# Two float32 products of an attention layer written as three split products each

## The chip, the cores and the metric

The kernel runs on one core of one Trainium2 chip. A time is the device time of one execution in microseconds, and what counts is the median of several runs. The profile is one execution of the same program, recorded by the hardware profiler; TensorE does the matrix products, VectorE, ScalarE and GpSimd the elementwise work, and SyncE issues most of the DMAs.

## The reference, cut to what matters

A sequence of 512 tokens with 16 learned meta tokens ahead of it (528 rows, width 2048) goes through two layers. Layer A is a gated linear recurrence. Layer B is forgetting attention with 16 heads of 128; its keys and values come from one projection of layer A's output. The change touches the part of layer B that follows:

```python
def fox_mix(h, g_norm, w_in, g_q, w_out, k, v, F, valid):
    u = rms_norm(h, g_norm) @ w_in
    q = rms_norm(u[..., :D_MODEL].reshape(bsz, L, FOX_HEADS, FOX_HDIM), g_q)
    z = u[..., D_MODEL:]
    ...
    for blk in range(Lp // Q_BLOCK):            # Q_BLOCK = 128
        s0 = blk * Q_BLOCK
        s1 = s0 + Q_BLOCK
        logits = jnp.einsum('bqhd,bkhd->bhqk', q[:, s0:s1], k[:, :s1]) * scale
        logits = logits + F[:, :, s0:s1, None] - F[:, :, None, :s1]
        logits = jnp.where(mask, logits, MASK_VALUE)
        p = jax.nn.softmax(logits, axis=-1)
        outs.append(jnp.einsum('bhqk,bkhd->bqhd', p, v[:, :s1]))
    ...
    return (o * jax.nn.silu(z)) @ w_out
```

All of it is float32.

## The kernel before

The kernel works with transposed activations: features on the 128 partitions, tokens along the free dimension. Its weights stream from HBM through `w_raw`, ScalarE rounds each piece to `w_hi` and VectorE subtracts to get `w_lo`, both in the type float32r, which is read as four bytes and takes one instruction for a product. A product in full accuracy is made of **three split products** that add up in PSUM: high x high, high x low, low x high. The activations have such a pair too (`sh`, `sl`). Everything large in the kernel is done so, in pieces of 256 to 512 moving columns. A product whose operands are plain float32 is recorded as two instructions.

Stages in time: layer A with its output projection, keys and values for layer B (to about 1405 us), the attention stage (to about 1826 us), and layer B's output projection. In the attention stage the projections for q and the gate z of head after head run through `run_ntiles`: for each of 32 slots 16 x 3 products of 512 columns (`pj`). Between them, in small pieces, stands the attention of an earlier head:

- `att_load` (L1672) loads kT (16+512 key columns) and the bias row Fb and, once the outputs of head h-2 are done, vtk and vc, which hold the values.
- `att_prep` (L1698) makes kh (ScalarE) and kl (GpSimd) of kT, the four masked bias tiles D (ScalarE, then GpSimd), the pair vh, vl of the values' first three blocks, and `v3`, a float32 copy of the fourth.
- `att_q` (L1723) scales the queries: the pair qh, ql for the query blocks 1 to 3, and `qg`, a float32 tile, for block 0; then the norms (`qy`).
- `att_blk` (L1765) does one query block i against its first 16 + 128(i+1) keys: scores into PSUM (`s`), bias (`lg`), softmax (`sm`, ScalarE's exponential), the transpose through DRAM (`py`, `pd`), and the parts PTh, PTl of the transposed weights. Block 0 has 144 columns, one float32 product of `qg` and kT. The blocks 1 to 3 have three split products for each piece of 272, 400, 272 and 256 columns.
- `att_o` (L1833) sums the outputs in PSUM (`o`): for each of three groups (vh x PTh, vl x PTh, vh x PTl) key blocks 0 to 2 against the query blocks that see them (512, 384 and 256 columns). The last key block meets only the last query block (128 columns): one float32 product of `v3` and `PT3`. A product with `vc` and Z adds the last 16 keys.

The order is written by a planner. All engines run what is issued to them in the written order. `do` writes an instruction only when a clock in the program, which adds up a price for each instruction, says that its operands are there; after each piece of a projection `tick` gives every waiting step a turn. In this clock a product of n columns costs TensorE 0.447 n + 3 ns in float32r and 1.9 n + 130 ns in float32, and from it comes where a step lands among the projections. When a slot begins that is two after a head's q slot, `att_o` of that head is put first in the list of steps.

All recorded instructions carry the line of a helper (L196), so rows are told apart by their tiles.

Of the kernel before, what the change touches and what calls it, by code (L numbers as in the profile page):

```python
# [14 lines left out]
P = 128  # L15
D = 2048
# [473 lines left out]
def trunk(  # L490
# [1207 lines left out]
    def att_prep(h):  # L1698
# [16 lines left out]
        while "vt" not in a:  # L1715
            yield
        a["v"] = yield from parts(a["vt"].rearrange("p (g b f) -> p g b f", g=4, f=32)[:, :, :3], "v", 384, ge, 2)
        v3 = tb.tile([P, P], F32, name="v3", tag="v3", bufs=2)
        yield from do(act, v3.rearrange("p (g f) -> p g f", f=32),
                      a["vt"].rearrange("p (g b f) -> p g b f", g=4, f=32)[:, :, 3], AF.Copy)  # L1720
        a["v3"] = v3

    def att_q(h, uq):  # L1723
# [7 lines left out]
        qh = tb.tile([P, 3 * P], F32R, name="qh", tag="qh")  # L1731
        ql = tb.tile([P, 3 * P], F32R, name="ql", tag="ql")
        yield from do(act, qh, uq[:, P:], AF.Identity, scale=g)
        yield from do(ve.scalar_tensor_tensor, ql, uq[:, P:], g, qh.bitcast(F32), ALU.mult, ALU.subtract)
        qg = tb.tile([P, P], F32, name="qg", tag="qg")
        yield from do(ge.tensor_scalar, qg, uq[:, :P], g, None, ALU.mult)
        free_u("buq")
        a.update(qg=qg, q=(qh, ql))
# [26 lines left out]
    def att_blk(h, i):  # L1765
        a = A[h]
        last = A.get(h - 1, {})
        kT, d = a["kT"], a["D"][i]
# [9 lines left out]
        for c0, c1 in cuts:  # L1778
            psS = ps.tile([P, 512], F32, name="s", tag="s", bufs=3)
            pss_.append(psS)  # L1780
            if i == 0:
                yield from do(te.matmul, psS[:, :n], lhsT=a["qg"], rhs=kT[:, :n], start=True, stop=True)
            else:
                qh, ql = (t[:, (i - 1) * P:i * P] for t in a["q"])
                kh, kl = (t[:, c0:c1] for t in a["k"])
                for j, (qq, kk) in enumerate(((qh, kh), (qh, kl), (ql, kh))):
                    yield from do(te.matmul, psS[:, :c1 - c0], lhsT=qq, rhs=kk, start=j == 0, stop=j == 2)
# [31 lines left out]
        if "PTh" not in a:  # L1819
            a["PTh"] = tb.tile([P, 4, 384], F32R, name="PTh", tag="PTh", bufs=1)  # L1820
            a["PTl"] = tb.tile([P, 4, 384], F32R, name="PTl", tag="PTl", bufs=1)
            a["PT3"] = tb.tile([P, P], F32, name="PT3", tag="PT3", bufs=1)
# [6 lines left out]
        if i == 3:  # L1829
            yield from do(act, a["PT3"].rearrange("p (g f) -> p g f", f=32), src[:, :, 3], AF.Copy)  # L1830
        a["fin"].add(i)

    def att_o(h):  # L1833
        a = A[h]
        while "v3" not in a or len(a["fin"]) < 4:
            yield
        PTh, PTl, PT3 = a["PTh"], a["PTl"], a["PT3"]
        while not all(te.matmul.fits((), {"lhsT": v, "rhs": w}) for v, w in (
                (a["v"][0], PTh), (a["v"][1], PTl), (a["v3"], PT3), (a["vc"], Z[h % 2]))):
# [270 lines left out]
```

## Time and profile before

| | us |
|---|---|
| median of 3 runs | 2013.81 |
| lowest, highest | 2009.59, 2014.51 |
| the profiled execution's own time | 2009.89 |
| its span, first to last instruction | 2008.2 |
| TensorE busy | 1980.4 |
| VectorE, ScalarE, GpSimd busy | 1573.1, 1000.5, 319.6 |
| granted TensorE clock, mean | 0.997 of 2.4 GHz |

The recorded duration of a product runs from its start to the end of its way through the array, and the next product starts long before that end. What a product costs is therefore read from start to start. Rows named PEld are loads of the stationary operand; one stands before each product.

### The profile page before, as it was taken

What the parts mean: (1) busy time and instruction counts of PE and PEld (TensorE: products, weight loads), DVE (VectorE), ACT (ScalarE), POOL (GpSimd) and SP (SyncE); (2) the same over time, 40 slices, a digit from 0 to 9 for tenths busy, and PEclk for the clock granted to TensorE, in tenths of its full rate; (3) what the DMA queues carried; (4) which work ended last, traced back from release to release, by engine and by line L of the source; (5) the groups of instructions that cost most, each with busy time, mean ns of one, the idle gap of its engine ahead of it and who ended that gap; (6) DMA issues with size and microseconds to landing.
All of it is one profiled execution on the core that took longest, in us unless ns stands there. A gap on an engine that the chain in (4) does not pass through costs nothing.

```text
span 2008.2 us, 39614 instructions
## 1 busy us (share of the span) xinstructions
PE 1980.4 (99%) x14604; PEld 1851.0 (92%) x14604; DVE 1573.1 (78%) x3153; ACT 1000.5 (50%) x1869; POOL 319.6 (16%) x429
## 2 busy tenths in 40 slices
PE   8999999999999999999999999999999999999999
PEld 7999999999999999889999999999788888887888
DVE  6878888888888887788788887868677777776965
ACT  6655454545454545544343333323666666666532
POOL 2121111111111111111210000000211111220011
PEclk9999999999999999999999999999999999999999
DMA  8343333434343433446563445446556555565552
GB/s 268 101 113 109 107 112 103 116 101 119 99 120 99 120 99 104 147 132 179 163 197 98 114 123 140 117 119 184 157 159 172 157 155 164 164 166 141 147 167 91
DMA packets 455492, 273.39 MB, mean 136 GB/s; under 512 B 78065, under 2 KB 420577, under 8 KB 455281
## 3 DMA queue, kind: packets, MB, share of 16 engines
q1 hardware_dynamic: 453728, 266.33, 46.6%
q0 software_dynamic: 1536, 4.52, 0.6%
q8 instruction: 115, 1.88, 0.4%
q14 instruction: 81, 0.66, 0.1%
q10 hardware_dynamic: 32, 0.01, 0.0%
HBM read 222.46 MB, written 48.28 MB: 135 GB/s over the span
## 4 chain that ended last, share of the span: by engine, by line
PE 80%; DVE 6%; DMA 5%; ACT 4%; issue 3%; SPq 2%; POOL 0%; ACTq 0%; DVEq 0%; POOLq 0%
PE pj L196 74%; SPq L196 2%; PE o L196 2%; DMA py<-pd 2%; PE tr L196 2%; PE pat L196 2%; DVE w_lo L196 1%; ACT w_hi L196 1%; DVE lg L196 1%; DVE sm L196 1%; DMA pd<-py 1%; DVE kl L196 1%; DMA w_raw<-in_a_w_in_dram 1%; ACT lg L196 1%; ACT D L196 1%
## 5 line engine op out<-in xcount | busy, mean ns | idle before, releaser
L196 PE MATMUL pj<-sh,w_hi 128*128 128x264 f32 (+1 forms) x2484 | 750.2, 315 | 5.2 <-ACT sh L196 2.2
L196 PE MATMUL pj<-sh,w_lo 128*128 128x264 f32 (+1 forms) x2484 | 732.5, 308 | 2.4 <-DVE w_lo L196 2.4
L196 PE MATMUL pj<-sl,w_hi 128*128 128x264 f32 (+1 forms) x2484 | 733.3, 308 | 1.5 <-DVE sl L196 1.5
L196 DVE TENSOR_TENSOR w_lo<-w_raw,w_hi 128x512 fp32r<-128x512 f32 x585 | 429.7, 743 | 84.2 <-ACT w_hi L196 82.3
L196 PEld LDWEIGHTS pj<-sh,w_hi 128*128 128x128 f32 x2484 | 456.8, 189 | 27.7 <-ACT sh L196 3.2
L196 PEld LDWEIGHTS pj<-sh,w_lo 128*128 128x128 f32 x2484 | 455.8, 189 | 24.8 <-DVE w_lo L196 3.1
L196 PEld LDWEIGHTS pj<-sl,w_hi 128*128 128x128 f32 x2484 | 456.6, 189 | 20.4 <-DVE sl L196 2.5
L196 ACT ACTIVATE w_hi<-w_raw 128x512 fp32r<-128x512 f32 x585 | 354.6, 621 | 146.2 <-PE pj L196 104.3
L196 PE MATMUL pj<-sm,w_hi 128*128 128x264 f32 x896 | 172.2, 289 | 0.0
L196 ACT ACTIVATE w_hi<-w_sum 128x512 fp32r<-128x512 f32 x120 | 74.5, 626 | 179.2 <-POOL w_sum L196 93.4
L196 PE MATMUL pj<-kh,w_lo 128*128 128x264 f32 x556 | 142.7, 285 | 0.8 <-DVE w_lo L196 0.8
L196 PE MATMUL pj<-kh,w_hi 128*128 128x264 f32 x556 | 143.5, 286 | 0.0
L196 PE MATMUL pj<-kl,w_hi 128*128 128x264 f32 x556 | 142.8, 285 | 0.0
L196 PEld LDWEIGHTS pj<-sm,w_hi 128*128 128x128 f32 x896 | 138.5, 188 | 1.4
L196 PE MATMUL pj<-sm,w_lo 128*128 128x264 f32 x448 | 127.6, 285 | 0.0
L196 POOL TENSOR_TENSOR w_sum<-w_sum,w_raw 128x512 f32<-128x512 f32 x34 | 51.8, 1522 | 456.0 <-DVE w_sum L196 252.6
L196 ACT ACT_TABLE_LOAD x88 | 112.9, 1283 | 5.9 <-issue 3.1
L196 DVE TENSOR_TENSOR w_lo<-w_sum,w_hi 128x512 fp32r<-128x512 f32 x120 | 90.3, 757 | 13.5 <-ACT w_hi L196 12.6
L196 PEld LDWEIGHTS pj<-kh,w_lo 128*128 128x128 f32 x556 | 98.4, 188 | 1.3 <-DVE w_lo L196 1.3
L196 PEld LDWEIGHTS pj<-kh,w_hi 128*128 128x128 f32 x556 | 98.4, 189 | 0.0
L196 PEld LDWEIGHTS pj<-kl,w_hi 128*128 128x128 f32 x556 | 98.3, 188 | 0.0
L196 PE MATMUL pj<-kh,sh 128*128 128x264 f32 x324 | 87.6, 286 | 0.0
(403 smaller groups left out, 3568.2 us busy)
## 6 DMA issues: line engine op xcount, KB each, us to landing
w_raw<-in_a_w_in_dram SPq DMA_DIRECT2D x256, 256.0 KB, 3.4
w_raw<-in_kv_w_dram SPq DMA_DIRECT2D x128, 256.0 KB, 4.1
w_raw<-in_b_w_in_dram SPq DMA_DIRECT2D x128, 256.0 KB, 3.3
w_raw<-in_a_w_out_dram SPq DMA_DIRECT2D x64, 256.0 KB, 3.8
w_raw<-in_b_w_out_dram SPq DMA_DIRECT2D x64, 256.0 KB, 3.9
xr<-xT SPq DMA_DIRECT2D x16, 264.0 KB, 3.7
h1T<-h SPq DMA_DIRECT2D x16, 264.0 KB, 2.1
kT<-kn SPq DMA_DIRECT2D x16, 264.0 KB, 2.4
```

The costliest lines, as they stand in the source:

```text
L196: ins = f(*args, **kw)
```

## The change

In the attention stage of layer B both float32 products become three split products. The query pair qh, ql now covers all 512 queries, and `qg` goes. The pair vh, vl covers all four value blocks, and the copy `v3` goes. `PT3`, the last key block's weights, becomes a pair PT3h (ScalarE) and PT3l (VectorE, a subtraction). The scores of block 0 take the same path as those of the other blocks, and each of the three groups of `att_o` ends with a product of 128 columns. The shapes of the results are the same.

```diff
         while "vt" not in a:
             yield
-        a["v"] = yield from parts(a["vt"].rearrange("p (g b f) -> p g b f", g=4, f=32)[:, :, :3], "v", 384, ge, 2)
-        v3 = tb.tile([P, P], F32, name="v3", tag="v3", bufs=2)
-        yield from do(act, v3.rearrange("p (g f) -> p g f", f=32),
-                      a["vt"].rearrange("p (g b f) -> p g b f", g=4, f=32)[:, :, 3], AF.Copy)
-        a["v3"] = v3
+        a["v"] = yield from parts(a["vt"].rearrange("p (g b f) -> p g b f", g=4, f=32), "v", 512, ge, 2)
...
-        qh = tb.tile([P, 3 * P], F32R, name="qh", tag="qh")
-        ql = tb.tile([P, 3 * P], F32R, name="ql", tag="ql")
-        yield from do(act, qh, uq[:, P:], AF.Identity, scale=g)
-        yield from do(ve.scalar_tensor_tensor, ql, uq[:, P:], g, qh.bitcast(F32), ALU.mult, ALU.subtract)
-        qg = tb.tile([P, P], F32, name="qg", tag="qg")
-        yield from do(ge.tensor_scalar, qg, uq[:, :P], g, None, ALU.mult)
+        qh = tb.tile([P, S], F32R, name="qh", tag="qh")
+        ql = tb.tile([P, S], F32R, name="ql", tag="ql")
+        yield from do(act, qh, uq, AF.Identity, scale=g)
+        yield from do(ve.scalar_tensor_tensor, ql, uq, g, qh.bitcast(F32), ALU.mult, ALU.subtract)
         free_u("buq")
-        a.update(qg=qg, q=(qh, ql))
+        a["q"] = qh, ql
...
-            if i == 0:
-                yield from do(te.matmul, psS[:, :n], lhsT=a["qg"], rhs=kT[:, :n], start=True, stop=True)
-            else:
-                qh, ql = (t[:, (i - 1) * P:i * P] for t in a["q"])
-                kh, kl = (t[:, c0:c1] for t in a["k"])
-                for j, (qq, kk) in enumerate(((qh, kh), (qh, kl), (ql, kh))):
-                    yield from do(te.matmul, psS[:, :c1 - c0], lhsT=qq, rhs=kk, start=j == 0, stop=j == 2)
+            qh, ql = (t[:, i * P:(i + 1) * P] for t in a["q"])
+            kh, kl = (t[:, c0:c1] for t in a["k"])
+            for j, (qq, kk) in enumerate(((qh, kh), (qh, kl), (ql, kh))):
+                yield from do(te.matmul, psS[:, :c1 - c0], lhsT=qq, rhs=kk, start=j == 0, stop=j == 2)
...
-            a["PT3"] = tb.tile([P, P], F32, name="PT3", tag="PT3", bufs=1)
+            a["PT3"] = [tb.tile([P, P], F32R, name=f"PT3{x}", tag=f"PT3{x}") for x in "hl"]
...
         if i == 3:
-            yield from do(act, a["PT3"].rearrange("p (g f) -> p g f", f=32), src[:, :, 3], AF.Copy)
+            hi, lo = (t.rearrange("p (g f) -> p g f", f=32) for t in a["PT3"])
+            yield from do(act, hi, src[:, :, 3], AF.Copy)
+            yield from do(ve.tensor_tensor, lo, src[:, :, 3], hi.bitcast(F32), op=ALU.subtract)
...
-        for m, (vv, pp) in enumerate(((vh, PTh), (vl, PTh), (vh, PTl))):
+        for m, (vv, pp, p3) in enumerate(((vh, PTh, PT3[0]), (vl, PTh, PT3[0]), (vh, PTl, PT3[1]))):
             for j in range(3):
                 c = slice(j * P, (j + 1) * P)
                 te.matmul(po[:, j * P:], lhsT=vv[:, c], rhs=pp[:, j:, c],
-                          start=j == 0 and m == 0, stop=m == 2 and j == 2)
+                          start=j == 0 and m == 0, stop=False)
+            te.matmul(po[:, 3 * P:], lhsT=vv[:, 3 * P:], rhs=p3, start=False, stop=m == 2)
             if m == 1:
-                te.matmul(po[:, 3 * P:], lhsT=a["v3"], rhs=PT3, start=False, stop=False)
                 te.matmul(c128(po)[:, :, P - NM:], lhsT=a["vc"], rhs=Z[h % 2][:, :, NM:],
                           start=False, stop=False)
```

The order of the instructions moves in the whole attention stage. On TensorE, in the last slot of the kernel before (gate of head 15), the second output group of head 14 and the first score product of head 15 stand among the projections (PT and v are the tiles `PT3` and `v3`):

```order
L196 MATMUL o<-PTh,vl 128x512
L196 MATMUL o<-PTh,vl 128x384
L196 MATMUL o<-PTh,vl 128x256
L196 MATMUL o<-PT_24255,v_24109 128x128
L196 MATMUL o<-Z_19231,vc 128x4x16
L196 MATMUL s<-kT,qg 128x144
L196 MATMUL pj_24330<-sh_19140,w_hi_24378 128x512
```

In the changed kernel the last slot has head 15's first scores, now three products, among the projections:

```order
L196 MATMUL pj_24361<-sh_18943,w_lo_24379 128x512
L196 MATMUL s<-kh,qh 128x144
L196 MATMUL s<-kl,qh 128x144
L196 MATMUL s<-kh,ql 128x144
L196 MATMUL pj_24361<-sh_19037,w_hi_24378 128x512
```

and head 14's first two output groups come behind the last projection and the last scores, directly ahead of the first product of the output projection (`pj_24562`):

```order
L196 MATMUL s<-kh,ql 128x256
L196 MATMUL o<-PTh,vh 128x512
L196 MATMUL o<-PTh,vh 128x384
L196 MATMUL o<-PTh,vh 128x256
L196 MATMUL o<-PT3h,vh 128x128
L196 MATMUL o<-PTh,vl 128x512
L196 MATMUL o<-PTh,vl 128x384
L196 MATMUL o<-PTh,vl 128x256
L196 MATMUL o<-PT3h,vl 128x128
L196 MATMUL o<-Z_19231,vc 128x4x16
L196 MATMUL pj_24562<-w_hi_24448,sh_24568 128x512
```

So one score product became three, one output product of 128 columns became one in each group, and head 14's outputs moved from the middle of the last slot to its end.

On ScalarE, at the same end of the stage, in the kernel before (`buz` is the gate's sigmoid, `sh` the first operands of the output projection):

```order
L196 ACTIVATE lg,sm<-lg,sm 128x272
L196 ACT_TABLE_LOAD
L196 ACTIVATE buz<-pj_24330 128x512
L196 ACTIVATE sh_24545<-g_19910 128x512
L196 ACTIVATE sh_24549<-g_20190 128x512
L196 ACTIVATE sh_24553<-g_20417 128x512
L196 ACTIVATE w_hi_24562<-w_raw 128x512
L196 ACT_TABLE_LOAD
L196 ACTIVATE lg,sm<-lg,sm 128x400
```

and in the changed one:

```order
L196 ACTIVATE lg,sm<-lg,sm 128x272
L196 ACT_TABLE_LOAD
L196 ACTIVATE buz<-pj_24361 128x512
L196 ACT_TABLE_LOAD
L196 ACTIVATE lg,sm<-lg,sm 128x400
L196 ACTIVATE lg,sm<-lg,sm 128x528
L196 ACTIVATE sh_24568<-g_19885 128x512
```

The exponentials of head 15's last two blocks and one table load moved ahead of the first `sh`.

## Rows read from the trace of the kernel before

**Rows 1.** The page: TensorE's busy time, and the chain by engine.

```profile
PE 1980.4 (99%) x14604; PEld 1851.0 (92%) x14604; DVE 1573.1 (78%) x3153; ACT 1000.5 (50%) x1869; POOL 319.6 (16%) x429
...
PE 80%; DVE 6%; DMA 5%; ACT 4%; issue 3%; SPq 2%; POOL 0%; ACTq 0%; DVEq 0%; POOLq 0%
```

**Rows 2.** Stretches: length, busy us (instructions) of PE, PEld, DVE, ACT, POOL; clock; DMA.

```profile
1405.00:1800.00 395.00, 391.96 (x1925) 321.44 (x1924) 291.46 (x688) 253.16 (x544) 75.65 (x166) 1.00 0.59 160
1800.00:1860.00 60.00, 56.99 (x264) 46.62 (x263) 42.18 (x91) 36.68 (x74) 4.16 (x10) 0.97 0.54 148
```

**Rows 3.** TensorE's waits, whole run: who, for whom, us in total, times, longest.

```profile
PE o L196 <- ACT PTh L196: 1.7, 3, 0.7
```

**Rows 4.** Groups by shape, 1405 to 1860 us: count, busy us, mean ns, idle before.

```profile
L196 PE MATMUL s<-kT,qg 128*128 128x144 f32 x32 | 6.7, 290 | 0.0
```

**Rows 5.** TensorE in order of time: start us, duration us; head 0's first scores.

```profile
1427.54 0.39 PE L196 MATMUL pj<-sh,w_lo 128*128 128x512 f32 x1
1427.77 0.41 PE L196 MATMUL s<-kT,qg 128*128 128x144 f32 x2
1427.91 0.49 PE L196 MATMUL pj<-sh,w_hi 128*128 128x512 f32 x1
1428.24 0.40 PE L196 MATMUL pj<-sl,w_hi 128*128 128x512 f32 x1
```

**Rows 6.** TensorE in order of time: head 14's last key block.

```profile
1820.29 0.39 PE L196 MATMUL o<-PT,v 128*128 128x128 f32 x2
1820.51 0.33 PE L196 MATMUL o<-Z,vc 128*128 128x64 f32 x2
```

**Rows 7.** TensorE in order of time: a float32 product of 17 columns in layer A.

```profile
306.85 0.29 PE L196 MATMUL tr<-part,group 128*128 128x17 f32 x2
306.99 0.37 PE L196 MATMUL pj<-sh,w_hi 128*128 128x264 f32 x1
307.20 0.28 PE L196 MATMUL pj<-sl,w_hi 128*128 128x264 f32 x1
307.32 0.28 PE L196 MATMUL pj<-sh,w_lo 128*128 128x264 f32 x1
```

**Rows 8.** TensorE in order of time: split score products of head 15's last block.

```profile
1825.46 0.28 PE L196 MATMUL s<-kh,ql 128*128 128x272 f32 x1
1825.58 0.28 PE L196 MATMUL s<-kh,qh 128*128 128x256 f32 x1
1825.70 0.28 PE L196 MATMUL s<-kl,qh 128*128 128x256 f32 x1
```

**Rows 9.** Groups by shape of the other engines, 1405 to 1860 us.

```profile
L196 POOL TENSOR_SCALAR qg<-buq,gqs 128x128 f32<-128x128 f32 x16 | 10.8, 673 | 79.4 <-ACT buq L196 79.2
L196 POOL TENSOR_TENSOR vl<-vtk,vh 128x384 fp32r<-128x384 f32 x16 | 16.2, 1014 | 6.6 <-ACT vh L196 3.4 <-DMA vc<-vcd 2.4
L196 ACT ACTIVATE v<-vtk 128x128 f32<-128x128 f32 x16 | 4.7, 294 | 0.0
L196 DVE SCALAR_TENSOR_TENSOR ql<-buq,gqs,qh 128x384 fp32r<-128x384 f32 x16 | 9.7, 609 | 0.3 <-ACT qh L196 0.3
L196 DVE TENSOR_TENSOR PTl<-py,PTh 128x128 fp32r<-128x128 f32 x16 | 5.7, 357 | 0.9 <-ACT PTh L196 0.7
```

**Rows 10.** TensorE in order of time, behind the attention stage; wait and releaser in brackets.

```profile
1828.54 0.51 PE L196 MATMUL pj<-w_hi,sh 128*128 128x512 f32 x1 [2.44 <-ACT sh L196]
...
1830.71 0.63 PE L196 MATMUL pj<-w_hi,sl 128*128 128x512 f32 x1
...
1833.70 0.50 PE L196 MATMUL pj<-w_hi,sh 128*128 128x512 f32 x1
```

**Rows 11.** ScalarE in order of time, at the same place.

```profile
1826.08 1.28 ACT L196 ACT_TABLE_LOAD   x1
...
1827.86 1.66 ACT L196 ACTIVATE sh<-g 128x512 fp32r<-128x512 f32 x3
...
1831.36 0.63 ACT L196 ACTIVATE lg<-lg,sm 128x400 f32<-128x400 f32 x1
```

More of the change, by code (lines that the diff above doesn't have):

```diff
@@ L1767, in att_blk @@
         last = A.get(h - 1, {})
-        kT, d = a["kT"], a["D"][i]
+        d = a["D"][i]
         n = NM + (i + 1) * P
@@ L1834, in att_o @@
         a = A[h]
-        while "v3" not in a or len(a["fin"]) < 4:
+        while "v" not in a or len(a["fin"]) < 4:
             yield
@@ L1838, in att_o @@
         while not all(te.matmul.fits((), {"lhsT": v, "rhs": w}) for v, w in (
-                (a["v"][0], PTh), (a["v"][1], PTl), (a["v3"], PT3), (a["vc"], Z[h % 2]))):
+                (a["v"][0], PTh), (a["v"][1], PTl), (a["v"][1], PT3[1]), (a["vc"], Z[h % 2]))):
             yield
```

## The prediction

> **What bounds the kernel now.** I read the busy time and the chain of waits first [rows 1]: TensorE is busy for 99% of the span, and 80% of the chain that ended last is TensorE work. The chain leaves few long gaps, so a product that is added or taken away on TensorE counts almost in full, and work on other engines counts only where TensorE waits for it. Next comes the table by stretches [rows 2]: in the attention stage, 1405 to 1800 us, TensorE is busy 391.96 of 395 us at the full granted clock (2.4 GHz), VectorE 74%, ScalarE 64%, GpSimd 19%. After that the list of waits [rows 3]: over the whole run the output products waited for their operand for 1.7 us in three places. So this stage has no slack on TensorE and plenty beside it. Only the end of the stage differs, and it has a part of its own below.
>
> **What the change does on TensorE.** Per head it takes away two float32 products: the scores of the first query block (128x144) and the outputs of the last key block (128x128). Each is recorded as two instructions; for the scores of 16 heads that makes 32 records [rows 4]. In their place come three split products of the same width each. All six stand inside the stream of projections, which fills TensorE, so their price is path.
>
> What the old ones cost is read from the starts of what stands around them, because recorded durations overlap. The score pair starts at 1427.77, one projection product follows within it, and the next one starts at 1428.24 [rows 5]: 0.47 us, less 0.23 for one projection product of 512 columns (from 1427.54 to 1427.77), is 0.24 us. The output pair starts at 1820.29 and the next product at 1820.51 [rows 6]: 0.22 us. Removed: 0.46 us a head.
>
> What the new ones cost, no row shows. Every split product of this trace has 256 columns or more; one of 272 columns takes 0.12 us from start to start and one of 256 also 0.12 [rows 8]. There are three ends to choose from.
> - By columns alone, 144/256 and 128/256 of 0.117 us are 0.066 and 0.059 us. Three of each: 0.20 and 0.18 us, 0.38 a head, so 0.08 less than before.
> - By the load of the stationary operand. The float32 pair with only 17 moving columns [rows 7] starts at 306.85; the second product after it starts at 307.20. That is 0.35 us, less 0.12 for the one projection product of 264 columns in between, so 0.23 for the pair: as much as the pair of 128 columns. Width no longer counts there; each 128x128 operand that is loaded takes about 0.115 us, hidden only behind a product that lasts as long. Six loads: 0.69 us a head, 0.23 more than before.
> - By the rate that products of this width have. The nearest rows in every other respect (same place, same width, same 128x128 operand, same four-byte elements) are the float32 ones themselves: 0.24 and 0.22 us. If a narrow split product is served at that rate, three of each are 0.72 and 0.66, 1.38 us a head, 0.92 more.
>
> I take the third. The rate of 256 columns in 0.12 us is shown for wide shapes only, and the rows nearest in shape are the float32 ones. The other two remain as bounds and rivals. Sum on TensorE: 16 x 0.92 = 14.7 us.
>
> A page speaks against this choice. The Trainium skill (FP8 and Floating Point Precision, TensorE Precision Notes) says that exact float32 takes four passes through the array and that the reduced form reads the four bytes and truncates them. The score pair agrees with the four passes: 4 x 144 columns at 2.4 GHz are 240 ns, beside 0.24 us measured. A split product would then need one pass, and the first or second end would hold; no run here shows a narrow one. The same skill (TensorE: Matmul & The Clock Gate, LDWEIGHTS) puts the load of 128 columns at 107 ns, and the 17-column pair agrees with 0.115 us each. By the two pages together the sum would be the second end's.
>
> **What the change does beside TensorE.** Per head GpSimd loses the scaled copy qg (673 ns) and its vl grows from 384 to 512 columns (1014 ns before, so about a third more, +0.34 us): GpSimd gets lighter. ScalarE loses the copy v (294 ns), and its copies qh and vh grow by a third of their width: about even. VectorE's ql grows from 609 ns by at most 0.2 us, and a new subtraction of 128x128 comes, like the one of that shape at 357 ns [rows 9]: 16 x 0.56 = 9 us more on an engine with about 26% of the stage free. I cost these at nothing. What hides them is the projection stream of 512-column products; if that cover were missing for VectorE the cost would be those 9 us at worst, and slower products on TensorE only give it more room. The first scores now need kl from GpSimd, which the float32 form did not. But their bias needs GpSimd's D, which stands behind kl in GpSimd's queue anyway, so the softmax of this block doesn't start later, and the matmul is written into TensorE's order only when the planner deems its operands ready. No DMA is added. The planner prices the new products by their columns, so the order of the stage shifts; where its price is too low, TensorE runs behind plan and finds operands earlier, not later.
>
> **The end of the stage.** In the kernel before TensorE waits 2.44 us for ScalarE's sh (the first operand of the output projection); after the pause, products of 512 columns start 0.43 us apart from 1830.71 to 1833.70, seven of them, where 0.23 is usual, which costs 1.4 us [rows 10]. The mean clock granted from 1800 to 1860 us is 0.97 [rows 2]: for part of this stretch the lower of its two levels, 1.2 GHz, behind the wait. In the new order ScalarE has a table load (1.28 us) and two exponentials (0.63 us for 400 columns, so some 0.75 for 528) between the gate's sigmoid and sh [rows 11]: 2.7 us more in front of sh. Against that the exponential of 272 columns comes six projection products (1.4 us) earlier than it did, so sh is late by about 1.3 us. TensorE has two of the three output groups of head 14 to do in that time (products of 512, 384 and 256 columns, by the price per column above 2 x 0.52 us, and the narrow ones), which before stood among the projections. These cancel: zero, between -3.8 us (the pause and the slow stretch vanish) and +2.7 us.
>
> **Sum.** The profiled execution took 2009.89 us, its span 2008.2. With 14.7 us that is 2024.6. The median of the three runs is 2013.81, 3.9 us above the profiled one, so for the median: 2013.8 + 14.7 = 2028.5, rounded to 2028.
>
> **Rivals.**
> - *The load of the operands is the limit.* Six loads a head, +0.23 us, 16 x 0.23 = 3.7 us: 2017.5. For it: the 17-column pair, and that all split products carry a load of their own. Against: the load's price is shown in float32 pairs only, not in the split form. This is also the result of the two pages quoted above.
> - *The column rate holds, and the kernel is not slower.* Mechanism: split products of 144 and 128 columns stream at the rate of the wide ones, with their loads fully hidden. 16 x -0.08 = -1.3 us: 2012.5. It decides as soon as the six narrow products cost under 0.46/6 = 0.077 us each. For it: the price per column is the same at 256, 272 and 512 columns. Against: the load of 0.115 us, which a product of 0.066 us cannot cover.
> - *The stage's end decides.* If ScalarE's queue lets sh out late, or the covered pause vanishes with the slow clock, 2.7 us more or 3.8 us less than each case. Alone it makes no case of its own; with the column rate it reaches 2008.7.
> - *VectorE takes the cover away.* 9 us more work there could all show up: 2037 on top of the forecast, 2026 on top of the loads. Against: 26% of its time is free here.
>
> **How the numbers follow.** Forecast 0.55, own range 2023 to 2034. Operand loads 0.31, range 2013.5 to 2021.5. Column rate 0.08, 2008.7 to 2015. Something else 0.06: VectorE or reordering slower 0.04, faster 0.02. A change under 0.3%, 6 us, can hardly be told from none here, so the borders are 2007.8 and 2019.9. Slower: 0.55, 0.03 out of the loads and 0.04, 0.62. Faster: 0.03. Same: the rest, 0.35. A range from 2013 to 2033 leaves out a little of the forecast's upper end, nearly all of the column rate and the rest, about 2 in 10.
>
> **What would show it.** In the profile after, the starts around the three narrow score products: 0.72 us for three if I am right, 0.35 by loads, 0.20 by columns; the output ones 0.66, 0.35, 0.18. TensorE's busy time should rise by some 14 us in the attention stage with no new waits there, and VectorE's by 9 us without ending a wait. The pause at the stage's end should stay at 2 to 4 us. The prediction is wrong if the narrow products start 0.12 us apart or closer, or if a new wait of TensorE above 5 us appears.

## The result and the profile after

The changed kernel took 2024.07 us (median of 6 runs, 2022.42 to 2026.02), the kernel before 2012.99 (6 runs, 2008.35 to 2014.51) on the same chip: a ratio of 1.0061, 95% interval 1.0048 to 1.0073. It is slower by 0.6%, some 12 us. The forecast of 2028 is 4 us off and the sign is right, but the sum behind it is not: of the 14.7 us forecast for the narrow products 3.4 are there, and the rest of the loss comes from places that I had costed at nothing.

The profiled executions are 2024.24 us (span 2022.5) after and 2009.89 (span 2008.2) before: 14.3 us apart in their spans. The medians are 11.1 us apart, since the profiled execution before lies 3.1 us under its median; the parts below add up to the 14.3. First the page (busy time, then the chain that ended last) answers [rows 1]:

```profile
PE 1989.0 (98%) x14636; PEld 1856.6 (92%) x14636; DVE 1586.0 (78%) x3169; ACT 1000.5 (49%) x1853; POOL 310.7 (15%) x413
...
PE 82%; DVE 5%; DMA 5%; ACT 3%; SPq 3%; issue 2%; POOL 0%; DVEq 0%; ACTq 0%; POOLq 0%
```

TensorE is busy 8.6 us longer in a span that is 14.3 us longer, and the chain is TensorE's as before. Next the table by stretches of the changed kernel (length; busy us and instructions of PE, PEld, DVE, ACT, POOL; granted clock; DMA share; GB/s), answering [rows 2], with one more stretch in the output projection behind:

```profile
1405.00:1800.00 395.00, 391.48 (x1932) 319.82 (x1931) 297.03 (x687) 249.20 (x519) 67.14 (x150) 1.00 0.59 160
1800.00:1860.00 60.00, 54.50 (x253) 44.92 (x252) 44.39 (x100) 35.78 (x73) 4.75 (x10) 0.94 0.53 147
...
1930.00:1960.00 30.00, 27.04 (x171) 24.73 (x170) 20.56 (x30) 12.74 (x23) 3.54 (x3) 0.94 0.52 157
```

The long stretch of attention looks like the one before. Around the end of the stage TensorE loses 2.5 us of busy time and the granted clock falls from 0.97 to 0.94; from 1930 to 1960, where the kernel before was busy for all 30.00 us at 1.00, TensorE idles 3 us and the clock is 0.94 as well.

TensorE's waits over the whole run (who waits for whom: us in total, times, longest), where [rows 3] had one row of interest:

```profile
PE pj L196 <- ACT sh L196: 6.3, 3, 4.2
...
PE pj L196 <- ACT w_hi L196: 2.2, 1, 2.2
...
PE s L196 <- POOL kl L196: 1.8, 2, 1.2
PE o L196 <- ACT PTh L196: 1.7, 2, 1.3
```

Three of these are new or larger: sh was 4.6 us, w_hi 0.6, and scores never waited for kl.

**Where the 14.3 us are.** I cut the span at TensorE's rows: the stage (from attention B's first projection product to the last gate product), its end (to the first product of the output projection) and the output projection (to the last product's start). In each I priced every product at the start-to-start time that undisturbed rows show for its shape (0.232 us for 512 columns, 0.117 for 256, 0.1125 for a narrow split product, 0.1215 and 0.111 for each record of the float32 pairs) and took out the gaps that the trace names. What is left over is products that run at the lower granted clock (1.6 us more than their price before, 4.5 after), and small differences at the gaps and elsewhere.

| us | stage | end | output projection | products | idle | left over |
|---|---|---|---|---|---|---|
| before | 425.6 | 4.1 | 175.1 | 594.9 | 6.1 | 3.9 |
| after | 428.5 | 8.4 | 182.2 | 598.3 | 12.7 | 8.2 |
| difference | 2.9 | 4.3 | 7.1 | 3.4 | 6.6 | 4.3 |

Some of head 14's outputs moved from the stage into the two parts behind it. So of the 3.4 us of products 1.7 lie in the stage, 0.9 in its end and 0.8 in the output projection. Of the 6.6 us of idle time 0.5 lie in the stage, 3.1 in its end and 3.1 in the output projection.

**The narrow products.** TensorE in order of time at head 0's first scores, after, answering [rows 5] (start us, duration us):

```profile
1428.17 0.39 PE L196 MATMUL pj<-sh,w_lo 128*128 128x512 f32 x1
1428.40 0.23 PE L196 MATMUL s<-kh,qh 128*128 128x144 f32 x1
1428.47 0.27 PE L196 MATMUL s<-kl,qh 128*128 128x144 f32 x1
1428.58 0.27 PE L196 MATMUL s<-kh,ql 128*128 128x144 f32 x1
1428.69 0.44 PE L196 MATMUL pj<-sh,w_hi 128*128 128x512 f32 x1
1428.97 0.39 PE L196 MATMUL pj<-sl,w_hi 128*128 128x512 f32 x1
```

From the first row to the last are 0.80 us; two products of 512 columns at 0.231 leave 0.34 for the three scores, 0.11 each. In the kernel before the same reckoning gave 0.24 for the float32 pair. The outputs show it too. At the end of the stage, after:

```profile
1830.31 0.22 PE L196 MATMUL o<-PT3h,vh 128*128 128x128 f32 x1
1830.36 0.74 PE L196 MATMUL o<-PTh,vl 128*128 128x512 f32 x3
1830.94 0.22 PE L196 MATMUL o<-PT3h,vl 128*128 128x128 f32 x1
```

From one narrow product to the next are 0.63 us, where the three wide products between them take 0.52 without it. The time from the narrow start to the next start is only 0.05, and alone it would look like the price by columns; the rest of the cost shows one product later: the projection product behind the scores above takes 0.28 us to the next start where 0.23 is usual. Over the run each of a head's three groups takes 0.638 us instead of 0.520: 0.12 for each narrow product as read there, 0.1125 as priced above, 0.34 a head in place of the 0.22 of the float32 pair. With 0.095 more for the scores and 0.115 for the outputs the change costs 0.21 us a head, 3.4 us for 16 heads.

**The end of the stage.** ScalarE, after, answering [rows 11]:

```profile
1829.09 0.52 ACT L196 ACTIVATE PTh<-py 128x384 fp32r<-128x384 f32 x1 [1.84 <-DMA py<-pd]
...
1829.72 0.51 ACT L196 ACTIVATE lg<-lg,sm 128x272 f32<-128x272 f32 x1
...
1830.34 1.28 ACT L196 ACT_TABLE_LOAD   x1
1831.63 0.60 ACT L196 ACTIVATE buz<-pj 128x512 f32<-128x512 f32 x1
1832.25 1.28 ACT L196 ACT_TABLE_LOAD   x1
1833.54 0.63 ACT L196 ACTIVATE lg<-lg,sm 128x400 f32<-128x400 f32 x1
...
1834.17 0.72 ACT L196 ACTIVATE lg<-lg,sm 128x528 f32<-128x528 f32 x1
...
1834.88 1.65 ACT L196 ACTIVATE sh<-g 128x512 fp32r<-128x512 f32 x3
```

and TensorE at the same place, answering [rows 10]:

```profile
1827.12 0.39 PE L196 MATMUL pj<-sh,w_lo 128*128 128x512 f32 x1
...
1829.67 0.80 PE L196 MATMUL o<-PTh,vh 128*128 128x512 f32 x3 [1.33 <-ACT PTh L196]
...
1835.55 0.79 PE L196 MATMUL pj<-w_hi,sh 128*128 128x512 f32 x1 [4.17 <-ACT sh L196]
...
1840.73 0.63 PE L196 MATMUL pj<-w_hi,sh 128*128 128x512 f32 x1
1841.16 0.56 PE L196 MATMUL pj<-w_lo,sh 128*128 128x512 f32 x1
```

ScalarE works in the order in which it was written. It stands still for 1.84 us at PTh, whose transfer is late, and everything behind it moves along: the exponential, the table load, the sigmoid that the last gate needs, a second table load, two more exponentials, and only then sh. TensorE waits twice, 1.33 and 4.17 us, and afterwards products of 512 columns start 0.43 us apart until past 1840, where 0.23 is usual: the lower of the two clock levels, 1.2 GHz.

**The output projection.** A hundred microseconds later TensorE waits again; VectorE's row and then TensorE's, after:

```profile
1942.66 0.69 DVE L196 TENSOR_TENSOR w_sum<-w_raw 128x512 f32<-128x512 f32 x1 [6.19 <-DMA w_raw<-in_b_w_out_dram]
```

```profile
1944.87 0.39 PE L196 MATMUL pj<-w_hi,so 128*128 128x256 f32 x1 [2.15 <-ACT w_hi L196]
1946.06 0.38 PE L196 MATMUL pj<-w_lo,so 128*128 128x256 f32 x1 [0.80 <-DVE w_lo L196]
...
1948.28 0.63 PE L196 MATMUL pj<-w_hi,so 128*128 128x256 f32 x2
1948.70 0.41 PE L196 MATMUL pj<-w_lo,so 128*128 128x256 f32 x1
```

From about 1947 to 1950.6 products of 256 columns stand 0.21 us apart (two of them 0.42) instead of 0.12. VectorE had waited 6.19 us for the raw weights. SyncE's queue of the changed kernel shows what the weights stand behind:

```profile
1891.90 0.39 SPq L196 DMA_DIRECT2D w_raw<-in_b_w_out_dram  x1
1899.06 1.53 SPq L196 DMA_DIRECT2D out_dram<-ot  x3
1900.68 0.94 SPq L196 DMA_DIRECT2D w_raw<-in_b_w_out_dram  x2
```

Between the first row and the second the queue is blocked for 6.8 us by a store whose tile VectorE hasn't added yet (its additions for these three stores start at 1898.35), and the weight loads stand behind it. In the kernel before the same place was blocked for 2.2 us:

```profile
1884.08 0.93 SPq L196 DMA_DIRECT2D w_raw<-in_b_w_out_dram  x2
1887.22 2.86 SPq L196 DMA_DIRECT2D out_dram<-ot  x3
```

### The profile page after: what moved, and what is told of

The parts are those of the page before. It is cut to its first block, busy times and chain, and to the rows that moved or that the text cites. A ratio compares the mean times of both kernels' runs of the same rounds, so it can differ in the third digit from the quotient of the medians.

```text
span 2022.5 us, 39686 instructions
## 1 busy us (share of the span) xinstructions
PE 1989.0 (98%) x14636; PEld 1856.6 (92%) x14636; DVE 1586.0 (78%) x3169; ACT 1000.5 (49%) x1853; POOL 310.7 (15%) x413
## 4 chain that ended last, share of the span: by engine, by line
PE 82%; DVE 5%; DMA 5%; ACT 3%; SPq 3%; issue 2%; POOL 0%; DVEq 0%; ACTq 0%; POOLq 0%
PE pj L196 75%; SPq L196 3%; PE o L196 2%; PE tr L196 2%; DMA py<-pd 2%; PE pat L196 2%; DMA w_raw<-in_b_w_out_dram 1%; DVE lg L196 1%; DVE w_lo L196 1%; PE s L196 1%; DMA vtk<-vd 1%; ACT lg L196 1%; ACT w_hi L196 1%; DVE py L196 1%; DMA w_raw<-in_a_w_in_dram 1%
## 5 line engine op out<-in xcount | busy, mean ns | idle before, releaser
L196 DVE TENSOR_TENSOR w_lo<-w_raw,w_hi 128x512 fp32r<-128x512 f32 x585 | 434.4, 751 | 92.4 <-ACT w_hi L196 89.3
L196 ACT ACTIVATE w_hi<-w_sum 128x512 fp32r<-128x512 f32 x120 | 74.4, 626 | 177.2 <-POOL w_sum L196 93.4
L196 PE MATMUL pj<-w_hi,sh 128*128 128x512 f32 (+1 forms) x232 | 84.5, 364 | 4.2 <-ACT sh L196 4.2
```

What stands on the lines that cost most here:

```text
L196: ins = f(*args, **kw)
```

## The experiments

Twelve kernels ran, in three batches on three chips, each batch beside runs of the kernel before on its chip; so kernels of different batches are compared by their ratios. The letters A, B and C are each expectation's own. The table gives the median, the ratio to before with its 95% interval, and the parts as above from the profiled execution. One profile is one execution, and executions of a kernel spread over some 5 us, so a part that differs by 1 to 2 us between two kernels says nothing. Some profiles are also long for their kernel: those of e2, e7 and e11 lie 3.9, 4.8 and 3.2 us above their medians, while the one of the kernel before lies 3.1 under its own. Their parts add up to more than the medians show.

| | median us | ratio, interval | stage | end | out. proj. | products | idle | left over |
|---|---|---|---|---|---|---|---|---|
| e1 priced as before | 2021.35 | 1.0040, 1.0027 to 1.0054 | 436.5 | 5.2 | 176.9 | 598.3 | 12.9 | 7.5 |
| e2 exponentials first | 2020.61 | 1.0043, 1.0030 to 1.0056 | 428.7 | 7.6 | 182.6 | 594.9 | 14.7 | 9.2 |
| e3 early operands, after | 2019.64 | 1.0038, 1.0024 to 1.0051 | 430.1 | 4.9 | 180.1 | 598.3 | 10.9 | 5.9 |
| e4 ladder (one run) | 2049.97 | none | 461.8 | 6.4 | 177.5 | 634.1 | 7.8 | 3.8 |
| e5 sh first | 2023.18 | 1.0056, 1.0043 to 1.0069 | 430.2 | 6.2 | 181.8 | 598.3 | 10.3 | 9.6 |
| e6 stores on GpSimd's queue | 2022.02 | 1.0046, 1.0034 to 1.0058 | 429.3 | 10.4 | 177.2 | 598.3 | 9.9 | 8.8 |
| e7 early operands, before | 2018.73 | 1.0032, 1.0020 to 1.0043 | 427.1 | 4.3 | 184.5 | 594.9 | 12.2 | 8.8 |
| e8 outputs alone | 2021.96 | 1.0050, 1.0038 to 1.0062 | 430.3 | 9.3 | 178.2 | 596.8 | 13.8 | 7.2 |
| e9 planner's price alone | 2028.34 | 1.0079, 1.0065 to 1.0092 | 436.0 | 4.8 | 182.0 | 594.9 | 16.4 | 11.5 |
| e10 e5 and e6 together | 2020.06 | 1.0043, 1.0031 to 1.0056 | 429.8 | 7.6 | 176.9 | 598.3 | 8.6 | 7.4 |
| e11 scores alone | 2017.85 | 1.0036, 1.0023 to 1.0049 | 425.0 | 9.0 | 182.1 | 596.4 | 12.1 | 7.5 |
| e12 before, stores on GpSimd's queue | 2012.51 | 1.0002, 0.9994 to 1.0011 | 429.3 | 4.8 | 175.2 | 594.9 | 9.0 | 5.5 |

**e4: what a narrow product costs.** In the first block of each head 20 extra products of 32 to 256 columns, each with its load, whose results are overwritten by the scores behind them:

```diff
+            if i == 0:
+                for w in (32, 64, 128, 192, 256):
+                    for r in range(4):
+                        args = dict(lhsT=a["q"][0][:, :P], rhs=a["k"][0][:, :w], start=True, stop=True)
...
+                            te.matmul(psS[:, :w], **args)
```

> The changed kernel with 20 more products per head ahead of the first scores, whose results are overwritten: qh against the first 32, 64, 128, 192 and 256 columns of kh, four of each width in a row, in the split type. From start to start: by the load of the operand (theory A) 0.11 us for 32, 64, 128 and 192 columns alike and 0.12 for 256; by columns alone 0.015, 0.03, 0.06, 0.085, 0.117; at the rate of float32 products (the forecast's term) 0.053, 0.107, 0.213, 0.32 and then 0.12. In total by theory A 16 x 20 x 0.112 = 36 us over the changed kernel, 2060 us; at the float32 rate 16 x 4 x 0.81 = 52 us, 2076; by columns 20 us, 2044.

TensorE, and then its weight loads, in order of time in that kernel:

```profile
1427.34 2.49 PE L196 MATMUL s<-kh,qh 128*128 128x32 f32 x21
1429.66 0.28 PE L196 MATMUL s<-kl,qh 128*128 128x144 f32 x1
```

```profile
1427.11 2.56 PEld L196 LDWEIGHTS s<-kh,qh 128*128 128x128 f32 x21
```

21 products take 2.32 us from start to start, 0.11 each, whatever their width. Over all heads the medians are 111 ns at 32 columns, 112 at 64, 114 at 128, 113 at 192, and 121 at 256. So the columns don't set the time up to 192 at least; they do only from about 256. The ladder doesn't vary the operand, and by itself it would fit a fixed price for every product as well. The kernel before has rows against that, in the norms of the queries, where eight products of 4 columns have operands of 128x32:

```profile
1418.84 0.40 PE L196 MATMUL pj<-sh,w_lo 128*128 128x512 f32 x1
1419.17 0.25 PE L196 MATMUL pj<-part,group 128*32 128x4 f32 x8
...
1419.68 0.39 PE L196 MATMUL pj<-sl,w_hi 128*128 128x512 f32 x1
```

From the first row to the last are 0.84 us; less two products of 512 columns that is 0.38 for all eight, under 0.05 each. So it is the load of the 128x128 operand that costs 0.11. The Trainium skill (TensorE: Matmul & The Clock Gate, LDWEIGHTS) gives a load as its columns divided by 1.2, in ns, which makes an estimate of 107 ns for 128 columns; the ladder's 111 to 114 ns agree within 7 ns. The total rose by 26 us over the changed kernel where 36 were expected (320 products at 0.113). Idle and left over fell together by 9 us; that the other engines had more time with more work on TensorE would explain it, but one run doesn't show it.

**e1: is it the planner's price?** The changed kernel, with a split product under 256 columns priced at a third of the float32 price, so that the three together are planned like the pair they replace:

```diff
+            if ins[0].dtype == F32R and n < 256:
+                return (1.9 * n + 130) / 3
             if ins[0].dtype == F32R:
                 return max(60, 0.447 * n + 3)
```

> The changed kernel with one number of the planner altered: a split product under 256 columns is priced at a third of what the float32 product of its width cost in the planner, so that the planner's clock, and with it nearly the order of the kernel before, comes back. All products and all work beside TensorE are those of the changed kernel. Theory A (the narrow products cost what the load of their operands costs, 0.112 us each, 16 x 0.22 = 3.6 us in all, and the rest of the measured +11 us is the changed order, most of it behind the attention stage): 2015 to 2018 us, ratio to before 1.001 to 1.0025, three narrow score products still 0.34 us, first output-projection product again 3.5 to 4.5 us behind the last gate product (changed kernel: 8.4). Theory B (the rest is the added work on VectorE and the scores' new need of kl, whatever the order): 2022 to 2025 us, ratio about 1.005.

Neither: 2021.35. The order of the kernel before didn't come back either. I counted in the traces how many projection products stand ahead of each of the 384 score and output products that both kernels have: in the changed kernel 62 stand where they did before and the mean shift is 6.4 projection products, in e1 34 and 8.0. So e1 is one more order of the same work and doesn't tell the order from the added work on the other engines. The end of the stage (5.2) and the output projection (176.9) went back nearly to what they were before, and the stage lost 8 us instead. Over the whole run its output products wait 4.0 us for PTh (1.7 in the changed kernel) and its scores 2.0 us for kl.

**e2: does the order of ScalarE cost anything by itself?** The kernel before, float32 products and all, with the exponentials of head 15's blocks written ahead of the first sh:

```diff
-    while z_left or NH - 1 in A and "ry" not in A[NH - 1]:
+    while z_left or NH - 1 in A and A[NH - 1].get("ex", 0) < 4:
         spin()
```

> The kernel before, with its float32 products, and one thing moved: the exponentials of head 15's last two blocks (and a table load) are written ahead of the first operands of the output projection on ScalarE, as the changed order has them. Theory A: the order alone costs time, 2 to 5 us at the stage's end, 2015 to 2018 us, ratio 1.001 to 1.0025, and the wait of the first output-projection product grows from 2.4 us by 2 to 4. Theory B: no more than 1 us, ratio 1.000.

It does: 0.43% slower with not one product changed, and more than the 2018 that I had allowed it. All 384 score and output products stand where they did before among the projections, so this is the cleanest of the orders. Its longest wait (columns as above) is the changed kernel's wait for sh over again:

```profile
PE pj L196 <- ACT sh L196: 7.9, 3, 5.7
```

The end took 7.6 us instead of 4.1, and the output projection 182.6 instead of 175.1, as in the changed kernel; of the 14 us by which this profile is longer the medians show some 8.

**e3 and e7: the operands of the output projection split early.** During the last gate product, in the changed kernel (e3) and in the kernel before (e7):

```diff
+    def early(k):
+        if k in (6, 9, 12):
+            movo.append(split_to_s1(len(movo), G[len(movo)], cols=S))
...
-        (pt,) = run_ntiles([("b", kind, h)], movb, 1)
+        (pt,) = run_ntiles([("b", kind, h)], movb, 1, early if slot == len(border) - 1 else None)
```

> The changed kernel, and the first three operands of the output projection are split during the last slot of the stage, as soon as their places are free, so that no exponential stands ahead of them. Theory A: the pause behind the stage (4.2 us of waiting and the slow products after it, some 7 to 8 us with the second half clock stretch) goes, 2014 to 2018 us, ratio 1.001 to 1.0025, since the 3.6 us of the narrow products stay. Theory B: the pause is not what costs, 2021 us or more.

> The kernel before, with the first three slices for the output projection split during the last gate product instead of behind it; float32 products as before. If the pause at the end of the stage (4.1 us before) is mostly the wait for those splits, it falls to under 2 us and the time from 2013 to 2010 to 2011. If ScalarE's and VectorE's other work there is only pushed behind them and then waited for, or the output projection pays as it did in the changed kernel, 2013 to 2016.

In the changed kernel it helps somewhat: 0.38% behind the kernel before instead of 0.61, between what the two theories asked for, and the end is down from 8.4 to 4.9. In the kernel before the same edit costs 0.32%: the wait for sh goes (idle at the end falls from 2.4 to 0.8 us), and the output projection rises to 184.5 in a profile that is 4.8 us above the median. I had expected a gain.

**e5: sh first, in the changed kernel.** The exponentials of head 15's last two blocks are held back until the first output projection product is written:

```diff
+        while h == NH - 1 and i > 1 and not held:
+            yield
         while not act.fits((lg, lg, sm), {}):
```

> The changed kernel, with the exponentials of head 15's last two query blocks held back until the first slices for the output projection are split, so that ScalarE splits them straight after the last gate's sigmoid; every product as in the changed kernel. Theory A (the order of ScalarE at the end of the stage is what the change costs beyond the 3.4 us of its products, there and through what it sets off behind it): the pause between the last gate product and the output projection falls from 8.4 to 5.8 us, the output projection from 182 to 177, and the time from 2024 to 2016 to 2018. Theory B (the loss in the output projection has a cause of its own, the weights queued behind the stores): only the 2.6 us of the pause come back, 2021 to 2022.

Theory A fell and B's 2021 to 2022 was missed a little: 2023.18, an interval that covers the changed kernel's ratio. In the profile the idle at the end falls from 5.5 to 2.1 us, but 1.7 us are left over there now, 1.2 of them at the lower clock, and the output projection still takes 181.8. So what that loses doesn't come from the pause at the end of the stage alone.

**e6 and e12: the stores off SyncE's queue.** One word, in the changed kernel (e6) and in the kernel before (e12):

```diff
-            yield from do(sy.dma_start, outv[:, b, n * 512:(n + 1) * 512], ot)
+            yield from do(ge.dma_start, outv[:, b, n * 512:(n + 1) * 512], ot)
```

> The changed kernel, with the stores of the first output columns issued from GpSimd's queue instead of SyncE's, so that no weight transfer stands behind a store that waits. Theory B (the weights of the output projection come late because they stand behind such stores): the wait for w_hi and w_lo near 1945 goes, the output projection falls from 182 to 177 to 178 us, and the time from 2024 to 2019 to 2020. Theory A (the loss there follows from the pause at the end of the stage, whichever queue stores): 2023 to 2025.

> The kernel before with the stores of the first output columns issued from GpSimd's queue. TensorE waits 0.6 us in its output projection, so the stores' place can give back next to nothing there: 2012 to 2013 if the loss is one of the changed kernel alone; under 2011 if the queue costs the kernel before as well.

The queue of GpSimd in e6 (wait and releaser in brackets), and then TensorE where the changed kernel had waited:

```profile
1901.73 1.74 POOL L196 DMA_DIRECT2D out_dram<-ot  x3 [7.02 <-DVE ot L196]
```

```profile
1944.97 0.28 PE L196 MATMUL pj<-w_hi,so 128*128 128x256 f32 x1
1945.09 0.28 PE L196 MATMUL pj<-w_lo,so 128*128 128x256 f32 x1
```

The store still waits 7 us for VectorE, but now nothing stands behind it, and both of TensorE's waits are gone: the output projection takes 177.2 instead of 182.2. Four later stores, which hold SyncE's queue for 4.6 us at 1930 in the changed kernel, stay on that queue in e6, so it is the earlier stores that count. The same holds for e10 against e5 (176.9 against 181.8). In the kernel before, where the block was short, the edit does nothing (ratio 1.0002). In the profile this part of the loss is shown. In the median it is not clear of the noise: e6 is 0.46% behind, against 0.61 with an interval that overlaps, and 2022 misses the 2019 to 2020 that theory B asked for; in the profiled execution the end of the stage was 2.0 us longer.

**e10: both repairs.**

> The changed kernel with both repairs: the slices for the output projection split ahead of the last exponentials, and the stores on GpSimd's queue. If the two losses are separate, the profile shows an end of 5 to 6 us and an output projection of 177 us, and the time is 2016 to 2018. If one repair's gain is handed on to another wait: 2020 to 2022.

2020.06: 0.43% behind the kernel before where the changed kernel is 0.61% behind, with intervals that overlap, at the near edge of "handed on to another wait". The output projection is mended. At the end the first score of a block now waits 1.2 us for a buffer that VectorE reads (lg) and the output products 1.4 for PTh, and the products behind run at the lower clock (0.91 granted from 1800 to 1860 us).

**e8 and e11: one part at a time.** Outputs alone (e8) is the changed kernel with the first block's scores put back to float32; scores alone (e11) has v3 and PT3 put back instead. The core of e8 against the changed kernel:

```diff
+            if i == 0:
+                yield from do(te.matmul, psS[:, :n], lhsT=a["qg"], rhs=kT[:, :n], start=True, stop=True)
+            else:
+                qh, ql = (t[:, (i - 1) * P:i * P] for t in a["q"])
```

and of e11:

```diff
+        v3 = tb.tile([P, P], F32, name="v3", tag="v3", bufs=2)
...
+            a["PT3"] = tb.tile([P, P], F32, name="PT3", tag="PT3", bufs=1)
...
+                te.matmul(po[:, 3 * P:], lhsT=a["v3"], rhs=PT3, start=False, stop=False)
```

> The outputs of the last key block as three split products, the scores of the first query block left in float32. By the load of operands (theory A) its products cost 1.9 us more than before; its order at the end of the stage again puts a table load and an exponential ahead of the split of the first slices, which by the run with that order alone costs 3 to 8 us: 2018 to 2023. If the order there were of no account: 2015.

> The scores of the first query block as three split products, the outputs of the last key block left in float32. Its products cost 1.5 us more than before. If the losses of the two parts add (outputs alone stood 9.3 us above before, both together 11), 2014 to 2015. If each is mostly a new order of the work around it, which comes once whichever part is changed: 2018 to 2022.

The products go by the load (+1.9 and +1.5 us), the times by more: 0.50% and 0.36%, 10 and 7 us, which together would be 17 where both in one kernel cost 12. The parts don't add; the difference is a little more than the intervals allow. e11 came out just under the 2018 expected for that case. Each one alone brings most of a loss that comes with a new order, in e8 as 8.2 us of idle at the end, in e11 as 5.6 us there and the late weights of the output projection.

**e9: a new order and nothing else.** The kernel before, with every product and every other instruction as it was; only the number by which the planner prices the two float32 products in attention B is lowered, from 0.40 and 0.37 us to 0.20 and 0.18, what it charges for the three split products in the changed kernel. The trace has the same instructions with the same shapes and counts as the one before. The order is not the changed kernel's but a third one: of the 384 products counted for e1, 62 stand where they do in the changed kernel.

```diff
+            if self.attention and n in (128, 144):
+                return 3 * (0.447 * n + 3)
             return max(60, 1.9 * n + 130 if outs[0].shape[0] > 64 else n + 20)
```

> The kernel before with every product unchanged; only the planner's price of the two float32 products of a head (first scores, last outputs) is lowered in attention B, from 0.40 and 0.37 us to what three split products are priced at, so that the planner weaves by the same numbers as in the changed kernel. ScalarE's order at the end of the stage stays that of before. Theory C (any other weaving of this stage than the one of before loses 5 us and more, whatever the products): 2017 to 2021. Theory A (it is the order at the end of the stage and the products that cost): 2012 to 2015.

2028.34, 0.79% slower, more than the change itself, and slower than theory C asked for. Its waits, and the stretch around the end of the stage (columns as above):

```profile
PE pj L199 <- ACT w_hi L199: 5.9, 6, 2.4
...
PE pj L199 <- ACT sh L199: 5.2, 3, 3.0
```

```profile
1800.00:1860.00 60.00, 54.27 (x235) 43.36 (x234) 42.05 (x98) 35.60 (x76) 6.96 (x17) 0.91 0.50 133
```

The longest wait for w_hi comes about like the one for sh in the changed kernel. ScalarE first, then TensorE:

```profile
1826.49 0.52 ACT L199 ACTIVATE PTh<-py 128x384 fp32r<-128x384 f32 x1 [6.43 <-DMA py<-pd]
1827.03 1.28 ACT L199 ACT_TABLE_LOAD   x1
...
1828.77 0.61 ACT L199 ACTIVATE w_hi<-w_raw 128x512 fp32r<-128x512 f32 x1
```

```profile
1829.43 0.50 PE L199 MATMUL pj<-sh,w_hi 128*128 128x512 f32 x1 [2.44 <-ACT w_hi L199]
```

PTh and a table load stand in front of a weight split, PTh's transfer is late, and the projection stream, which has nothing to do with it, runs dry. With equal products, 10.3 us more of idle and 7.6 us more left over (3.4 of them at the lower clock) make up the whole 18 us by which the three parts together are longer than before.

## Why the prediction was right in its number and wrong in its sum

- **"I take the third" is the step that failed.** The narrow split product was taken at the float32 rate, 0.24 and 0.22 us each, +14.7 us in all. It takes 0.11 us and the sum is +3.4. The rival that I gave 0.31 had this term right (0.115 each, +3.7 us). I ranked rows by likeness of shape. The 17-column pair, farther away in shape, showed the mechanism: it cost as much as the pair of 128 columns, so time there doesn't go by columns. The two pages of the Trainium skill named in the prediction gave this result too, and the ladder agrees with the load.
- **The column rate** (0.066 us a product) is out: at 32 columns a product still takes 0.111 us.
- **"These cancel: zero" was wrong.** sh was put 1.3 us late, because the exponential of 272 columns stands six projection products earlier than before. Earlier in the order was not earlier in time: it stood behind PTh, which waited 1.84 us for its transfer. In the kernel before sh started 3.4 us after the start of the last gate product, in the changed kernel 7.8, so it is 4.3 us late, and the end grew by as much, 3.1 of it idle time. My upper bound was 2.7.
- **"The order of the stage shifts" was passed over in one sentence** and turned out to be the larger part of the loss. I argued only that a price too low makes TensorE run behind plan and so finds operands earlier. e9 has that price without the products that take longer, and loses 16 us; e2 moves a few instructions at the end and loses 8. The sentence was about the cover of TensorE's operands; what is lost is in the queues beside it, where one late item holds up those written behind it.
- **The output projection** had no term at all. It lost 7.1 us in the profile, 0.8 of it products that moved there, and e6 gives 5 back in its profile.
- **Work beside TensorE at nothing: held, but for kl.** VectorE's busy time rose by 13 us over the run, and from 1405 to 1800 by 5.6; its added work is 6.7 us (ql 737 ns for 609, and 290 for PT3l, in 16 heads), where I had 9. No wait of TensorE for VectorE grew by that. The first scores do wait for kl, 1.8 us in two places, where I had said no later: the point on D covers the softmax behind the product, not TensorE itself.
- **What would show it.** I named starts 0.12 us apart as the sign that the prediction is wrong, and that is what the rows show. "TensorE's busy time up by 14 us in the stage with no new waits": the stage grew by 2.9 us, and there are new waits. "The pause at the end stays at 2 to 4 us": it is 5.5.

So two errors of opposite sign: 11.3 us too much for the products, and 10.9 too little for idle TensorE and what follows it (by the medians, which are 11.1 us apart, 7.7 too little). The time fell into the range by their sum, which was luck, and not by the argument.

What stays open: even with both repairs (e10) the kernel is 0.43% behind, and of these 8.7 us the products are 3.4. The rest is spread over small waits in the stage and at its end. That the order alone can cost this much is shown by e2 and e9; that in the changed kernel all of it is the order is not, since no run here has its added work on VectorE, ScalarE and GpSimd in the order of before. I didn't find an order of the changed kernel that is as good as the one the kernel before has, and an order planned with the measured 0.113 us was not run. No kernel here beats the one before; e12 ties with it.

## What to carry to other kernels

A split product with a 128x128 operand of its own costs its load, 0.11 us here, however few columns move. Three of them cost 0.34 us, more than the float32 pair of 0.22 to 0.24 us that they replace. Whether they pay at larger widths was not measured here. Where a planner's prices set the order, cost the new order as a term of its own and bound it from both sides; a control that changes the prices and not the work (e9) shows for the price of one kernel what a new order can cost.

## What I had not expected of the hardware

- The time per product is flat from 32 to 192 columns (111 to 114 ns), and 256 columns take 121.
- An idle TensorE costs more than the idle time in the trace. In the changed kernel 6.6 us of added idle came with 4.3 us more left over, and 2.9 of these are products at the lower clock: after the two pauses shown above, products stand at nearly double spacing until past 1840 and until 1950.6 us (0.43 for 0.23, 0.21 for 0.12). In e9 10.3 us of idle came with 7.6, 3.4 of them at the lower clock. A further part stands at the pauses themselves: the trace counts idle time from the recorded end of a product, for 512 columns 0.39 us after its start, while the next one would have started after 0.23.
- A store that waits in SyncE's queue reached TensorE some 45 us later, through the weights behind it. Taking the stores out of that queue gave back 5 us in the profiles of both kernels where it mattered (the changed one and e5). The output projections of e2, e9 and e11 are as long (182 us) and wait for w_hi as well, and SyncE's queue is blocked for the same 6.8 us at the same place in all three; in e1 it is 2.2 us, as before, and the part takes 176.9. e5 doesn't fit this: the block there is 1.5 us and the part takes 181.8, so which store holds the weights up in e5 stays open.
